# Moving the second half's convolution beside the first half's attention, with three projection panels taken out of that stage

## The chip, the cores and the metric

The kernel runs on one core of a Trainium2 chip. The metric is the device time of one launch in microseconds (us): the median of the runs of the kernel before is 1644.02 us, over three runs from 1640.84 to 1645.38. The profile is that of one further execution, with a time of 1639.46 us.

## The reference, cut to what matters

One layer of a decoder over 1024 tokens of width 1024, in float32, with three sub-layers. Only the parts that the change touches are written out.

```python
def reference(x, mem, ...):
    mem_n = rms_norm(mem, mem_norm_g)
    # 1. two mixers side by side, from one projection
    p = rms_norm(x, g[0]) @ w_in                       # 1024 -> 1024 + 1792 columns
    y_conv = conformer_conv(p[..., :1024])             # gate, causal conv of width 31, layer norm, silu
    y_rwkv = rwkv7_mix(p[..., 1024:])                  # token shift, then a recurrence over tokens
    x = x + rms_norm(concat([y_conv, y_rwkv]) @ w_out, g[1])
    # 2. attention of 4 heads into 256 memory tokens
    x = x + rms_norm(memory_cross_attention(rms_norm(x, g[2]), mem_n, wq, wkv, wo), g[3])
    # 3. channel mixer
    return x + rms_norm(swiglu(rms_norm(x, g[4]), w_gu, w_down), g[5])

def conformer_conv(u):
    h = u[..., :512] * sigmoid(u[..., 512:])
    h = causal_depthwise_conv(h, conv_w) + conv_b      # 31 taps per channel
    return silu(layer_norm(h, ln_g, ln_b))
```

## The kernel before, in words

**Halves.** The tokens are worked on in two halves of 512. `run` (from L955) writes the stages of half 0 (projection, mixers, attention), then those of half 1, with the channel mixer of half 0 as filler in half 1's stages, and last the channel mixer of half 1.

**Matmuls.** Every large product is made of three matmuls, of a high and a low part of each operand (`mm3`, L197). Each weight tile of 128x1024 is loaded into a ring of four `wraw` tiles (L177), ScalarE makes the high part `whi` (L171), and VectorE (or GpSimd where `pool_share` is above 0) makes the low part `wlo` (L172); `whi` and `wlo` have two tiles each, so weights are used in the order in which the program asks for them. `feat` (L203) makes one 128x512 tile `psf` with 24 matmuls; `tokmajor` (L212) makes four tiles `pst` at a time.

**Projection panels.** `w_in_block` (L300) takes a list of panels, each of two such `psf` tiles. The convolution's panels (4, 0, 6, 2) gate their columns and write them to `hd` in DRAM (L332). The other mixer's panels (20, 12, 8, 16, 14, 10, 18) go through `evq` (L311 to L324) to `pdr`.

**The convolution.** `conv_taps` (L341) loads 128 channels of `hd` into `hin` (two tiles), makes the first tap on ScalarE (L349) and thirty more: for three of the four channel groups on VectorE (L356), for group 0 with a product on ScalarE (L353) and a sum on GpSimd (L354). `conv_norm` (L361) is the layer norm and the silu, with the results written to `yd` (L398).

**Order.** The instructions of each engine stand in an order that is fixed when the program is built: a scheduler with costs of its own takes what is ready, what comes earlier in the program first, so a later instruction that is ready goes into a gap. `weave(main, side, rate)` (L53) puts steps of `side` between those of `main` in the program, in proportion to the numbers that both yield. `fill(us)` (L784) takes steps of `self.filler` until their numbers have used up the credit. In half 0, `self.filler` holds the seven mixer panels of half 1, and gets a credit of 6 at the load before the output projection, 6 for each of the four token tiles of a `residual` (L763), and 5 before the transposes of the attention; a step of it counts 5.2.

**Stages around the change.** In the mixers' stage of half 0 the recurrence's `rwkv_chain` is followed by `memory_maps` (L823), the norm of half 1, and half 1's convolution panels, woven with half 0's convolution. Then come `mix_out` and `attention` of half 0, with the panels as filler. After that half 1 has `rwkv_prep` (L422), `rwkv_inverse` (L592: 31 dependent steps, GpSimd for the first 20 rows and VectorE for the rest, L621 and L622), and `rwkv_chain` (L652); half 1's convolution is woven into the channel mixer of half 0 behind them (L1054). A `residual` with a next norm scales and adds (L772), squares on ScalarE (L253), takes a root on GpSimd (L239), scales again (L265), and `transposed` (L271) makes the pairs `nextT` that the next stage's matmuls read.

Of the kernel before, what the change touches and what calls it, by code (L numbers as in the profile page):

```python
# [9 lines left out]
F32 = mybir.dt.float32  # L10
F32R = mybir.dt.float32r
AF = mybir.ActivationFunctionType
# [5 lines left out]
P = 128  # L18
# [3 lines left out]
TB = 512  # L22
# [30 lines left out]
def weave(main, side, rate):  # L53

    lag = 0.0
    for us in main:
        yield us
        lag += us * rate
        while lag > 0.0:
            lag -= next(side, 1e9)  # L60
    drain(side)


def drain(*gens):
    for g in gens:
        for _ in g:
            pass


class Trunk:  # L70
    def __init__(self, ctx, tc, x, mem, cols, lora, gpost, w_in, w_out, wqT, wkv, wo, w_gu, w_down, out):
# [5 lines left out]
        nc = self.nc  # L77
# [46 lines left out]
        nc.gpsimd.memset(self.mhalf, -0.5)  # L124
        self.carry = cp.tile([P, 14], F32, name="carry")
        nc.gpsimd.memset(self.carry, 0.0)
        pad = cp.tile([P, 40], F32, name="pad")
        nc.gpsimd.memset(pad, 0.0)

        def derive(name, n, src, mul, add):  # L130
            t = cp.tile([P, n], F32, name=name)
            nc.vector.tensor_scalar(t, src, mul, add, op0=ALU.mult, op1=ALU.add)
            return t
        col = self.col
# [6 lines left out]
        nc.vector.tensor_scalar(self.cwh, self.cwh, 0.5, None, op0=ALU.mult)  # L141
        self.lgh = derive("lgh", 4, col("ln_g"), 0.5, 0.0)
        self.lbh = derive("lbh", 4, col("ln_b"), 0.5, 0.0)


        self.pool_share = self.share = 0.0
# [18 lines left out]
    def col(self, name, i=None, n=1):  # L165
        a, b = COLS[name]
        return self.cols[:, a:b] if i is None else self.cols[:, a + i:a + i + n]
# [172 lines left out]

    def conv_taps(self, b, pool, acc):  # L341
        nc = self.nc
        t0 = b * TB
        for j in CONV_ORDER:
            h = pool.tile([P, 576], F32, tag="hin", bufs=2, name="hin")[:, 0:TB + CONVW - 1]
            nc.sync.dma_start(out=h, in_=self.hd[j * P:(j + 1) * P, t0:t0 + TB + CONVW - 1])
            a = acc[:, j, :]
            w = lambda k: self.cwh[:, j * CONVW + k:j * CONVW + k + 1]
            nc.scalar.activation(out=a, in_=h[:, 0:TB], func=AF.Identity, scale=w(0), bias=self.col("conv_b", j))  # L349
            for k in range(1, CONVW):  # L350
                if j == CONV_POOL:
                    p = pool.tile([P, TB], F32, tag="t", bufs=2, name="tap")
                    nc.scalar.activation(out=p, in_=h[:, k:k + TB], func=AF.Copy, scale=w(k))  # L353
                    nc.gpsimd.tensor_tensor(out=a, in0=a, in1=p, op=ALU.add)  # L354
                else:
                    nc.vector.scalar_tensor_tensor(out=a, in0=h[:, k:k + TB], scalar=w(k), in1=a,  # L356
                                                   op0=ALU.mult, op1=ALU.add)
                if k % 6 == 0:
                    yield 4.0

    def conv_norm(self, b, pool, acc):  # L361
        nc = self.nc
        t0 = b * TB
        tmp = lambda name: pool.tile([P, TB], F32, tag="t", bufs=2, name=name)
        add = lambda out, x, y: nc.vector.tensor_tensor(out=out, in0=x, in1=y, op=ALU.add)
        sa, sb = tmp("lnsa"), tmp("lnsb")
        add(sa, acc[:, 0, :], acc[:, 1, :])
        add(sb, acc[:, 2, :], acc[:, 3, :])
        add(sa, sa, sb)
        ps = self.pn.tile([P, TB], F32, tag="n", name="psln")  # L370
        nc.tensor.matmul(ps, self.ones, sa, start=True, stop=True)
        for j in range(4):
            nc.vector.scalar_tensor_tensor(out=acc[:, j, :], in0=ps, scalar=-1.0 / DR, in1=acc[:, j, :],
                                           op0=ALU.mult, op1=ALU.add)
        yield 6.0
        sa = tmp("lnsq")
        nc.scalar.activation(out=sa, in_=acc[:, 0, :], func=AF.Square)
        for j in range(1, 4):
            sb = tmp("lnsq")
            nc.scalar.activation(out=sb, in_=acc[:, j, :], func=AF.Square)  # L380
            add(sb, sa, sb)
            sa = sb
        ps = self.pn.tile([P, TB], F32, tag="n", name="psln2")
        nc.tensor.matmul(ps, self.ones, sa, start=True, stop=True)
        rs = pool.tile([P, TB], F32, tag="hin", bufs=2, name="lnrs")
        nc.vector.tensor_scalar(rs, ps, 1.0 / DR, LN_EPS, op0=ALU.mult, op1=ALU.add)
        ry = pool.tile([P, TB], F32, tag="hin", bufs=2, name="lnry")
        self.rsqrt(ry, rs, pool.tile([P, TB], F32, tag="t", bufs=2, name="lnt"))
        yield 6.0
        for j in range(4):  # L390
            a = acc[:, j, :]
            nc.vector.tensor_tensor(out=a, in0=a, in1=ry, op=ALU.mult)
            th = pool.tile([P, TB], F32, tag="t", bufs=2, name="lnth")
            sc, bi = self.lgh[:, j:j + 1], self.lbh[:, j:j + 1]
            nc.scalar.activation(out=th, in_=a, func=AF.Tanh, scale=sc, bias=bi)
            nc.scalar.activation(out=a, in_=a, func=AF.Identity, scale=sc, bias=bi)
            nc.vector.scalar_tensor_tensor(out=a, in0=th, scalar=1.0, in1=a, op0=ALU.add, op1=ALU.mult)
            nc.sync.dma_start(out=self.yd[j * P:(j + 1) * P, t0:t0 + TB], in_=a)  # L398
            yield 2.0
# [555 lines left out]
    def run(self):  # L955
        tc = self.tc
        L, R = "left", "right"
        opened = {}

        def push(name, side):  # L960
            opened[name] = tc.tile_pool(name=name, bufs=1, side=side, reuse_waits="tile")
            return opened[name].__enter__()

        def pop(*names):
            for n in names:
                opened.pop(n).__exit__(None, None, None)
# [5 lines left out]
        conv_cols, mix_cols = (4, 0, 6, 2), (20, 12, 8, 16, 14, 10, 18)  # L972
# [5 lines left out]
        ev = push("ev", R)  # L978
        mk = push("mk", R)
        a0 = push("a0", R)  # L980
        h0, h1, mT = self.pairs(a0), self.pairs(a1), self.pairs(mk, MEM, "m")
# [22 lines left out]
        kp = push("conv0", L)  # L1004
# [10 lines left out]
        def next_norm():  # L1015
            for t in range(0, 4, 2):
                self.normed(self.x, TB, (t, t + 2), h1, "g_mix", 2, (self.pd, "d"))
                yield 1.0 * 2
        maps = self.memory_maps(mT, ev, kv)
        w1 = self.w_in_block(1, h1, ev, conv_cols)  # L1020
        main = chain(islice(maps, 16), next_norm(), islice(w1, 0), maps, w1)
        drain(weave(main, self.conv(0, kp), 1.0))
        pop("mix0", "gn0", "conv0", "tt0", "xb", "kv", "mk")
        self.filler = self.w_in_block(1, h1, ev, mix_cols)

        yp = push("y0", L)
        a2 = push("a2", L)
        self.xn = 3
        self.xp = push("xc", R)
        ap = push("pc", R)  # L1030
        drain(self.mix_out(0, a2, yp))
        drain(self.attention(0, self.nextT, a2, yp, ap))
        self.fill(1e9)
        pop("pc", "xc")
        pop("ev", "a1")

        ya, ss = self.ya_tiles(yp), self.sums()
# [4 lines left out]
        pop("prep1")  # L1042
        tp = push("tt1", R)
        TT = tp.tile([P, NCH * HP, CH], F32, tag="TT", name="TT")
        kp = push("conv1", R)
        pp = push("inv1", R)
        self.rwkv_values(1, pp)
        self.rwkv_inverse(1, pp, TT)
# [1 line left out]
        gp = push("gn1", R)  # L1050
        mp = push("mix1", R)
        self.rwkv_chain(1, mp, gp, TT)
        side = self.conv(1, kp)
        self.filler = weave(self.filler, side, 1.5)  # L1054
        self.fill(270.0)
        drain(side)
        pop("mix1", "gn1", "conv1", "tt1")
        self.pool_share = 0.3
        a3 = push("a3", R)
        y1 = push("y1", R)  # L1060
# [2 lines left out]
        ap = push("pd1", R)  # L1063
# [72 lines left out]
```

## Time and profile before

| what | value |
|---|---|
| median of three runs | 1644.02 us (1640.84 to 1645.38) |
| profiled execution: its own time | 1639.46 us |
| profiled execution: its span, first to last instruction | 1637.7 us |
| mean granted clock of TensorE | 0.966 |
| TensorE matmul busy | 1537.0 us, 94% of the span |
| VectorE, ScalarE, GpSimd busy | 1056.9, 721.7, 369.3 us |

"Busy" is the share of time in which an engine has at least one instruction under way. For TensorE it does not say how fast it works: its granted clock is 1.0 (2.4 GHz) or 0.5 (1.2 GHz), and a stretch's mean tells how long it stood at the lower level. So a stretch's loss on TensorE is read as its idle time, plus the length times (1 - clock).

### The profile page before, as it was taken

The numbers are of one execution on the slowest core, as the hardware profiler recorded it, in microseconds if no ns is written. First come the engines' busy times: TensorE is split into PE (matmuls) and PEld (weight loads), VectorE is DVE, ScalarE is ACT, GpSimd is POOL, SyncE is SP. The second block draws the span as 40 slices with busy tenths as digits, with TensorE's granted clock in tenths as the row PEclk, the third lists the DMA queues.
The fourth block names the chain that finished last, engine by engine and source line by source line (L and its number), as shares of the span: only waits on it lengthen the run. The fifth ranks groups of instructions, "written<-read, shape, count | busy, mean of one in ns | idle before, by whom it ended". The sixth has DMA issues, their size and how long they took to land.

```text
span 1637.7 us, 22825 instructions
## 1 busy us (share of the span) xinstructions
PE 1537.0 (94%) x8688; PEld 1256.5 (77%) x8688; DVE 1056.9 (65%) x1501; ACT 721.7 (44%) x1122; POOL 369.3 (23%) x347
## 2 busy tenths in 40 slices
PE   7999867879999999999979889999999999999997
PEld 6777756767787888777758667878887788888886
DVE  5687698997545546768789997536537624343435
ACT  5654335867434434654224555534435332222222
POOL 1032390740000000022561730012113211111111
PEclk9999976889999999999999889999999999999999
DMA  6576967466636236457844235446236632323221
GB/s 203 174 222 202 280 210 230 123 201 224 223 130 204 96 109 191 143 161 225 245 129 136 94 113 168 136 141 206 90 94 230 229 101 92 103 90 103 90 90 52
DMA packets 175644, 257.37 MB, mean 157 GB/s; under 512 B 68912, under 2 KB 110000, under 8 KB 175536
## 3 DMA queue, kind: packets, MB, share of 16 engines
q1 hardware_dynamic: 174576, 255.08, 49.1%
q8 instruction: 68, 1.11, 0.3%
q10 hardware_dynamic: 960, 0.85, 0.2%
q14 instruction: 40, 0.33, 0.1%
HBM read 196.58 MB, written 59.31 MB: 156 GB/s over the span
## 4 chain that ended last, share of the span: by engine, by line
PE 44%; DVE 5%; POOL 4%; issue 2%; DMA 1%; ACT 1%; SPq 0%; POOLq 0%; DVEq 0%; ACTq 0%
PE psf L201 7%; PE psf L199 7%; PE psf L200 7%; PE pst L199 6%; PE pst L200 6%; PE pst L201 6%; DVE acc L356 2%; POOL tm L621 1%; POOL Tt L622 1%; DVE wlo L172 1%; PE psg L528 1%; DMA At<-sc 0%; DVE ya L921 0%; POOL rstd L239 0%; POOL wlo L172 0%
## 5 line engine op out<-in xcount | busy, mean ns | idle before, releaser
L171 ACT CAST whi<-wraw 128x1024 fp32r<-128x1024 f32 x256 | 268.0, 1049 | 533.8 <-PE psf L200 182.6
L201 PE MATMUL psf<-ahi,wlo 128*128 128x512 f32 (+1 forms) x1200 | 462.6, 386 | 26.2 <-DVE wlo L172 25.1
L199 PE MATMUL psf<-ahi,whi 128*128 128x512 f32 (+1 forms) x1200 | 460.7, 385 | 8.1 <-ACT whi L171 8.1
L200 PE MATMUL psf<-alo,whi 128*128 128x512 f32 (+1 forms) x1200 | 460.3, 384 | 0.0
L172 DVE TENSOR_TENSOR wlo<-wraw,whi 128x1024 fp32r<-128x1024 f32 x223 | 285.9, 1283 | 253.4 <-ACT whi L171 251.9
L201 PEld LDWEIGHTS psf<-ahi,wlo 128*128 128x128 f32 x1200 | 231.5, 193 | 74.7 <-DVE wlo L172 30.3
L199 PEld LDWEIGHTS psf<-ahi,whi 128*128 128x128 f32 x1200 | 231.7, 193 | 53.0 <-ACT whi L171 10.0
L200 PEld LDWEIGHTS psf<-alo,whi 128*128 128x128 f32 x1200 | 231.8, 193 | 42.7 <-issue 1.2
L172 POOL TENSOR_TENSOR wlo<-wraw,whi 128x1024 fp32r<-128x1024 f32 x33 | 79.8, 2417 | 554.4 <-ACT whi L171 497.6
L356 DVE SCALAR_TENSOR_TENSOR acc<-hin,cols,acc 128x512 f32<-128x512 f32 x180 | 164.3, 941 | 0.7
L200 PE MATMUL pst<-wlo,ahi 128*128 128x512 f32 x384 | 150.2, 391 | 1.4 <-POOL wlo L172 0.9
L201 PE MATMUL pst<-whi,alo 128*128 128x512 f32 x384 | 148.4, 391 | 0.0
L199 PE MATMUL pst<-whi,ahi 128*128 128x512 f32 x384 | 135.6, 395 | 2.5 <-ACT ahi L282 2.1
L200 PE MATMUL pst<-wlo,fhi 128*128 128x512 f32 x352 | 137.8, 392 | 0.1
L201 PE MATMUL pst<-whi,flo 128*128 128x512 f32 x352 | 134.3, 390 | 0.0
L199 PE MATMUL pst<-whi,fhi 128*128 128x512 f32 x352 | 134.0, 393 | 0.0
L239 POOL TENSOR_TENSOR rstd<-rstd,mhalf 128x1 f32<-128x1 f32 x50 | 34.5, 699 | 386.2 <-DVE rstd L238 376.9
L354 POOL TENSOR_TENSOR acc<-acc,tap 128x512 f32<-128x512 f32 x60 | 99.4, 1656 | 85.6 <-ACT tap L353 82.0
L921 DVE TENSOR_TENSOR ya<-pst,ya 128x512 f32<-128x512 f32 x80 | 54.3, 687 | 51.9 <-PE pst L201 51.8
L199 PEld LDWEIGHTS pst<-whi,ahi 128*128 128x128 f32 x384 | 71.6, 188 | 18.2 <-ACT ahi L282 2.6
L200 PEld LDWEIGHTS pst<-wlo,ahi 128*128 128x128 f32 x384 | 72.1, 188 | 16.8 <-POOL wlo L172 1.2
L201 PEld LDWEIGHTS pst<-whi,alo 128*128 128x128 f32 x384 | 71.8, 188 | 14.5
(244 smaller groups left out, 2006.5 us busy)
## 6 DMA issues: line engine op xcount, KB each, us to landing
wraw<-in_w_gu_dram SPq DMA_DIRECT2D x88, 512.0 KB, 3.6
wraw<-in_w_in_dram SPq DMA_DIRECT2D x44, 512.0 KB, 4.5
wraw<-in_w_down_dram SPq DMA_DIRECT2D x44, 512.0 KB, 3.6
wraw<-in_wkv_dram SPq DMA_DIRECT2D x16, 512.0 KB, 5.1
am<-amd SPq DMA_DIRECT2D x16, 512.0 KB, 5.3
wraw<-in_w_out_dram SPq DMA_DIRECT2D x16, 512.0 KB, 4.1
wraw<-gd SPq DMA_DIRECT2D x16, 512.0 KB, 4.4
wraw<-vwd SPq DMA_DIRECT2D x16, 512.0 KB, 3.4
```

What stands on the lines that cost most here:

```text
L171: self.nc.scalar.copy(out=hi, in_=src)
L172: (eng or self.nc.vector).tensor_tensor(out=lo, in0=src, in1=hi.bitcast(F32), op=ALU.subtract)
L199: mm(ps, w[0], x[0], start=start, stop=False)
L200: mm(ps, w[0], x[1], start=False, stop=False)
L201: mm(ps, w[1], x[0], start=False, stop=stop)
L239: nc.gpsimd.tensor_tensor(r, r, self.mhalf, op=ALU.pow)
L354: nc.gpsimd.tensor_tensor(out=a, in0=a, in1=p, op=ALU.add)
L356: nc.vector.scalar_tensor_tensor(out=a, in0=h[:, k:k + TB], scalar=w(k), in1=a, op0=ALU.mult, op1=ALU.add)
L528: nc.tensor.matmul(pg[g][:, i, :], bk[half[g], c + i, :], aq[half[g], :, c + i, :], start=True, stop=True)
L621: eng.tensor_tensor(out=w, in0=a, in1=c, op=ALU.mult)
L622: eng.tensor_tensor(out=u, in0=u, in1=w, op=ALU.add)
L921: nc.vector.tensor_tensor(out=y, in0=ps, in1=y, op=ALU.add)
```

## The change

- Half 1's convolution is written beside `mix_out` and `attention` of half 0, as the side of a `weave` with a rate of 0.7, and no longer behind half 1's `rwkv_chain`. Its pool `conv1` is opened on the right after `pc`, and closed with it.
- Its bias columns come from a new tile `cb` (128x8: `conv_b`, and the halved bias of the layer norm) in the constant pool, with one slot under the tag `convb`. Half 0's copy is made at the start by two VectorE copies; half 1's copy is made by two ScalarE copies at the head of `conv_taps(1)`, and its slot comes free with the last instruction of half 0's convolution that reads the bias (L395 and L396). The first tap (L349) of half 1 needs it. The `pad` tile shrinks by the same eight columns.
- The first three mixer panels of half 1 (20, 12, 8) are written behind the convolution's panels in the mixers' stage; the filler of the attention stage keeps four panels (16, 14, 10, 18). An `islice(w1, 0)` that took nothing goes.
- The filler in half 1's chain stage is now the channel mixer alone, with the same credit of 270.

```diff
+        self.cb = cp.tile([P, 8], F32, tag="convb", name="convb0")
+        nc.vector.tensor_copy(out=self.cb[:, 0:4], in_=col("conv_b"))
+        nc.vector.tensor_copy(out=self.cb[:, 4:8], in_=self.lbh)
...
     def conv_taps(self, b, pool, acc):
+        if b == 1:
+            self.cb = self.cp.tile([P, 8], F32, tag="convb", name="convb")
+            nc.scalar.copy(out=self.cb[:, 0:4], in_=self.col("conv_b"))
+            nc.scalar.copy(out=self.cb[:, 4:8], in_=self.lbh)
...
-            nc.scalar.activation(out=a, in_=h[:, 0:TB], func=AF.Identity, scale=w(0), bias=self.col("conv_b", j))
+            nc.scalar.activation(out=a, in_=h[:, 0:TB], func=AF.Identity, scale=w(0), bias=self.cb[:, j:j + 1])
...
-            sc, bi = self.lgh[:, j:j + 1], self.lbh[:, j:j + 1]
+            sc, bi = self.lgh[:, j:j + 1], self.cb[:, 4 + j:5 + j]
...
-        main = chain(islice(maps, 16), next_norm(), islice(w1, 0), maps, w1)
+        w1m = self.w_in_block(1, h1, ev, mix_cols[:3])
+        main = chain(islice(maps, 16), next_norm(), maps, w1, w1m)
...
-        self.filler = self.w_in_block(1, h1, ev, mix_cols)
+        self.filler = self.w_in_block(1, h1, ev, mix_cols[3:])
...
-        drain(self.mix_out(0, a2, yp))
-        drain(self.attention(0, self.nextT, a2, yp, ap))
+        kp = push("conv1", R)
+        def blocks():
+            yield from self.mix_out(0, a2, yp)
+            yield from self.attention(0, self.nextT, a2, yp, ap)
+        drain(weave(blocks(), self.conv(1, kp), 0.7))
         self.fill(1e9)
...
         self.rwkv_chain(1, mp, gp, TT)
-        side = self.conv(1, kp)
-        self.filler = weave(self.filler, side, 1.5)
         self.fill(270.0)
-        drain(side)
```

## Rows read from the trace of the kernel before

**Rows 1.** Busy us, share, instructions; granted clock in tenths, 40 slices

```profile
PE 1537.0 (94%) x8688; PEld 1256.5 (77%) x8688; DVE 1056.9 (65%) x1501; ACT 721.7 (44%) x1122; POOL 369.3 (23%) x347
...
PEclk9999976889999999999999889999999999999999
```

**Rows 2.** By stretch: length, then PE, PEld, DVE, ACT, POOL busy; clock; DMA

```profile
800.00:825.00 25.00, 23.09 (x106) 18.73 (x104) 24.79 (x43) 6.77 (x9) 22.96 (x26) 1.00 0.68 240
825.00:850.00 25.00, 17.07 (x72) 12.90 (x70) 20.08 (x21) 5.34 (x7) 20.67 (x28) 0.98 0.30 95
850.00:875.00 25.00, 24.22 (x367) 18.94 (x368) 24.00 (x34) 11.76 (x20) 0.00 (x0) 0.89 0.58 134
875.00:900.00 25.00, 25.00 (x203) 20.02 (x202) 21.39 (x33) 9.69 (x14) 4.44 (x3) 1.00 0.50 159
900.00:925.00 25.00, 20.75 (x147) 16.24 (x145) 24.79 (x21) 13.43 (x22) 18.40 (x13) 0.93 0.25 80
925.00:950.00 25.00, 19.42 (x109) 14.83 (x107) 24.83 (x24) 17.27 (x26) 20.08 (x12) 0.82 0.35 106
950.00:975.00 25.00, 21.50 (x132) 16.75 (x131) 24.38 (x32) 9.05 (x16) 6.72 (x5) 0.84 0.44 137
975.00:1000.00 25.00, 25.00 (x186) 19.56 (x185) 19.32 (x31) 17.37 (x25) 0.00 (x0) 1.00 0.35 111
...
1350.00:1375.00 25.00, 25.00 (x112) 20.71 (x111) 9.43 (x10) 6.53 (x9) 2.39 (x1) 1.00 0.30 101
```

**Rows 3.** The same view, of half 0's attention stage and of the GpSimd taps

```profile
410.00:690.00 280.00, 278.18 (x1290) 227.55 (x1289) 155.28 (x256) 126.74 (x209) 11.36 (x21) 1.00 0.48 156
...
895.00:957.00 62.00, 51.10 (x349) 39.67 (x347) 61.09 (x54) 38.31 (x58) 49.60 (x30) 0.89 0.30 93
```

**Rows 4.** VectorE's groups from 850 to 895 us: count, busy us, mean ns, idle before

```profile
L356 DVE SCALAR_TENSOR_TENSOR acc<-hin,cols,acc 128x512 f32<-128x512 f32 x36 | 25.1, 743 | 0.0
L172 DVE TENSOR_TENSOR wlo<-wraw,whi 128x1024 fp32r<-128x1024 f32 x7 | 8.5, 1221 | 7.9 <-ACT whi L171 7.9
```

**Rows 5.** The same view from 895 to 957 us, VectorE and then GpSimd

```profile
L356 DVE SCALAR_TENSOR_TENSOR acc<-hin,cols,acc 128x512 f32<-128x512 f32 x24 | 30.9, 1290 | 0.4
L172 DVE TENSOR_TENSOR wlo<-wraw,whi 128x1024 fp32r<-128x1024 f32 x5 | 10.1, 2013 | 0.0
...
L742 DVE TENSOR_TENSOR Y<-Y,yrr 128x512 f32<-128x512 f32 x1 | 1.8, 1778 | 0.0
...
L937 DVE SCALAR_TENSOR_TENSOR ftg<-ftg,psf 128x512 f32<-128x512 f32 x2 | 1.3, 674 | 0.0
...
L354 POOL TENSOR_TENSOR acc<-acc,tap 128x512 f32<-128x512 f32 x30 | 49.6, 1655 | 59.6 <-ACT tap L353 57.6
```

**Rows 6.** Who waited for whom, 790 to 865 us: total, times, longest

```profile
ACT Tn L625 <- POOL Tt L622: 10.4, 1, 10.4
...
PE psf L199 <- ACT whi L171: 5.4, 1, 5.4
```

**Rows 7.** The inverse's sums on GpSimd; half 1's taps: min/median/max ns, first and last start

```profile
L622 POOL TENSOR_TENSOR Tt<-Tt,tm x31: 250/657/1504, 796.7 to 847.5; 128x60 f32<-128x60 f32 x2, 128x220 f32<-128x220 f32 x2, 128x240 f32<-128x240 f32 x2, 128x247 f32<-128x247 f32 x2
...
L356 DVE SCALAR_TENSOR_TENSOR acc<-hin,cols,acc x90: 735/746/1829, 809.4 to 965.9; 128x512 f32<-128x512 f32 x90
```

**Rows 8.** The panels' evictions from 608 to 656 us: ns, first and last start

```profile
L311 ACT ACTIVATE evq<-psf,omu x7: 676/682/684, 616.3 to 651.8; 128x512 f32<-128x512 f32 x7
```

**Rows 9.** VectorE in order of time behind the attention: start us, us, idle before

```profile
609.54 1.28 DVE L772 SCALAR_TENSOR_TENSOR ya<-ya,rstd,xres 128x1024 f32<-128x1024 f32 x1
...
630.49 0.75 DVE L265 TENSOR_SCALAR ya<-ya,rstd 128x1024 f32<-128x1024 f32 x1 [0.60 <-POOL rstd L239]
```

**Rows 10.** TensorE in order of time there: last product of the attention

```profile
609.72 0.39 PE L201 MATMUL pst<-whi,alo 128*128 128x512 f32 x1
```

**Rows 11.** Half 1's gated columns written, and the convolution's last bias reader

```profile
L331 DVE SCALAR_TENSOR_TENSOR evh<-tg,psf x4: 679/680/681, 403.5 to 431.1; 128x512 f32<-128x512 f32 x4
...
L396 ACT ACTIVATE acc<-acc,lbh,lgh x4: 798/803/816, 400.7 to 406.3; 128x512 f32<-128x512 f32 x4
```

More of the change, by code (lines that the diff above doesn't have):

```diff
@@ L126, in __init__ @@
         nc.gpsimd.memset(self.carry, 0.0)
-        pad = cp.tile([P, 40], F32, name="pad")
+        pad = cp.tile([P, 32], F32, name="pad")
         nc.gpsimd.memset(pad, 0.0)
@@ L1030, in run @@
         ap = push("pc", R)
-        drain(self.mix_out(0, a2, yp))
-        drain(self.attention(0, self.nextT, a2, yp, ap))
+        kp = push("conv1", R)
[3 more added lines that the diff above has]
+        drain(weave(blocks(), self.conv(1, kp), 0.7))
         self.fill(1e9)
-        pop("pc", "xc")
+        pop("conv1", "pc", "xc")
         pop("ev", "a1")
@@ L1044, in run @@
         TT = tp.tile([P, NCH * HP, CH], F32, tag="TT", name="TT")
-        kp = push("conv1", R)
         pp = push("inv1", R)
@@ L1052, in run @@
         self.rwkv_chain(1, mp, gp, TT)
-        side = self.conv(1, kp)
-        self.filler = weave(self.filler, side, 1.5)
         self.fill(270.0)
-        drain(side)
-        pop("mix1", "gn1", "conv1", "tt1")
+        pop("mix1", "gn1", "tt1")
         self.pool_share = 0.3
```

## The prediction, made before the change was run

> **What bounds the kernel now.** I read the busy time first: TensorE is busy for 94% of the span, and its granted clock is below full only around slices 6 to 9 and 23 to 24 [rows 1]. So the time is TensorE's work plus what it loses, and a change that moves other engines' work is worth what TensorE loses in one place less what it loses in the other. The view by stretch gives the losses, as idle time plus length times (1 - clock). In a steady stretch 112 matmuls of 512 columns pass in 25 us without loss, 0.223 us each (1350 to 1375 us) [rows 2], so a `psf` of 24 takes 5.4 us. Half 1's taps on VectorE run from 809 to 966 us [rows 7]. In these stretches the loss is 1.9, 8.4 and 3.5 us from 800 to 875, 0 from 875 to 900, 6.0, 10.1 and 7.5 us from 900 to 975, and 0 after that, where the chain goes on with no taps [rows 2]: 13.8 us beside the inverse and 23.6 us in the chain. Half 0's attention, where the convolution is put, loses next to nothing: TensorE is busy for 278.2 of 280 us at full clock, VectorE for 155.3, GpSimd for 11.4 [rows 3].
>
> The view by lines then tells why the taps cost what they cost. From 850 to 895 us VectorE runs 36 taps of 743 ns each without a break, GpSimd does nothing, and TensorE loses little [rows 2, 4]. From 895 to 957 us GpSimd makes its 30 sums of channel group 0, VectorE has not 1 us to spare, and its taps take 1290 ns, its `wlo` 2013 instead of 1221 ns [rows 3 to 5]. Taps alone are cheap; taps beside GpSimd's sums are not.
>
> **What goes.** (1) The chain stage, 23.6 us. Without the convolution VectorE has there what it has from 975 us on (19.3 of 25 us busy, loss 0), so nearly all comes back. I leave 2 us for the chain's own hops: 21.5 us, between 17 and 23.6. The matmuls of the filler that stay are the same, by the same credit.
> (2) The inverse, 13.8 us from 800 to 875. Its end holds up ScalarE's copy `Tn` for 10.4 us, `whi` queues behind that copy, and TensorE waits 5.4 us for it [rows 6]. GpSimd's steps reach 1504 ns there at a median of 657 [rows 7], and the taps begin in the midst of them; without taps I expect the steps to be shorter and most of the loss to go: 9 us, between 5 and 13.
> Together 30.5 us, between 22 and 36.6.
>
> **What comes.** (3) The convolution beside the attention. VectorE gets 90 taps of 0.74 us and some 21 instructions of the norm of about 0.68 us (as the `psf` reader's 674 ns [rows 5]): 81 us, on 140 of 280 us (155.3 less, by my estimate, 15 for half 1's preparation, which begins at the end of that stretch [rows 3]). ScalarE, with 126.7 of 280 us busy, has room for 30 products and some 20 instructions more. That fits, as long as GpSimd's sums don't stretch it. From 895 to 957 us they did: 24 taps x 0.547 = 13.1, 5 `wlo` x 0.792 = 4.0, and the chain's own two-input work, by my estimate nine or ten instructions' worth at about 1.1 (1778 against some 690 ns), 10: some 27 us for 30 sums, or 0.9 us a sum [rows 4, 5]. The attention has taps and `wlo` but no chain: at least 13.1 + 4.0 = 17 us, at most 27; I take 20. TensorE lost 23.6 us for those 27 by 975 us, and 10.9 + 0.11 x 62 = 17.7 us within 895 to 957 [rows 2, 3], so 0.66 to 0.88 per us: 13 to 18 us. As scores and outputs need only `wlo` and an eviction in time, and no hops of a chain, I take 15. The ends: 0, where VectorE's free half hides it all, and 24, where the price moves with the taps.
>
> Here a rule has to be weighed. While GpSimd adds, the VectorE instructions that read PSUM keep their 674 ns; those with two inputs in SBUF stretch [rows 5]. The Trainium skill says the same (SBUF — State Buffer, section "SBUF: two separate sides"): the port pair of the two engines is an exclusive lock for a whole instruction, for a VectorE instruction with two SBUF inputs against one of GpSimd's that reads SBUF. At the ceiling of that lock, where each sum blocks VectorE for its whole 1655 ns [rows 5], 30 sums take 50 us from it, term (3) is 33 in place of 15, and the sum +19.5, 1663 us. The rows show 0.9 us a sum, and they decide.
>
> (4) The held tile. Its two ScalarE copies wait for the last bias reader, which is ScalarE's own (L396, start 406.3 us) [rows 11], so what is queued behind them (`whi`, evictions) waits for nothing that it did not wait for already. Two copies of 4 columns at the start and two here: 0, at most 1 us. Half 1's gated columns are written from 403.5 to 431.1 us [rows 11], so the taps can begin near 413 us, in VectorE's gaps, and GpSimd's sums once one `hin` is free, by my estimate near 460 to 480 us; before that the taps stand alone, as in rows 4. The loads of `hin` and the writes of `yd` go through SP's queue with the weights' loads; late taps delay those, which is inside the 0.66 to 0.88.
>
> (5) The three panels. Their six `psf`, 6 x 5.4 = 32 us of TensorE, leave the attention stage and go to the end of the mixers' stage, where TensorE has no idle time to fill: 0 by themselves. But they were cover. Of the 14 panel tiles seven are evicted only behind the attention's last product [rows 8], which ends at 610.1 us [rows 10]. What hides behind those seven is the second `residual`: four rounds of scale, add, square, root and scale, the first at 609.5, the last at 630.5 us and over at 631.2 [rows 9], some 21 us; then a transpose and a copy, 1 us. The channel mixer's first matmul needs that result. The credit counts by steps of 5.2: two tiles for the load, four in the first `residual`, one before the transposes, and the eighth in the second `residual`. With 14 tiles that left seven, as seen; with 8 it leaves one, 5.4 us. Half 1's preparation can't fill in: its tiles take the place of `h1` and `ev`, which the eighth tile still reads. So TensorE stands from about 615.5 to between 629 (rounds of 4.6 us by my estimate, with less to share the engines with) and 632 us: 14 to 16.5 us, and one or two more at 1.2 GHz, as behind the idle time at 825 to 850 us [rows 2]. I take 16, between 9 and 20. This is new; the first `residual` keeps its four tiles.
> (6) Late rounds in that first `residual`, if taps stand between its steps: 1, between 0 and 5.
>
> **The sum.** -21.5 - 9 + 15 + 0 + 16 + 1 = +1.5 us on the profiled execution's 1639.46 us, hence 1641.0; the median of the runs is 4.56 us above that execution, so 1645.5, say 1646 us.
>
> **Rivals.**
> A, the forecast: gains and new losses about cancel; 1636 to 1655 by (3) and (5) within 5 us of what I took. For it: each term has a row. Chance 0.42.
> B, faster: the attention absorbs the taps. Its VectorE is half idle and much of its work reads PSUM, which GpSimd doesn't slow [rows 3, 5]; then (3) is 3 and (6) 0, and the sum is -21.5 - 9 + 3 + 16 = -11.5: 1632 us. If the rounds also get shorter (5 at 9), 1625. Against it: the scheduler packs taps into every gap, so where the sums run, VectorE may be as full as at 895 us. Chance 0.30.
> C, slower: GpSimd's sums meet VectorE's taps and the first `residual` in the attention at the old price. Place: the 50 to 60 us of the sums; price 24, and 5 for (6); the sum is -30.5 + 24 + 16 + 5 = +14.5: 1658 us. It decides slower from (3) + (6) of 20 us on (30.5 - 16 + 5). For it: the same 30 sums and 90 taps, and an order of instructions made beforehand, which can't step aside. Against: no chain. With a full block by each sum, as weighed under (3), it would be 1668, 0.03 of the chance. Chance 0.23.
> D, the change doesn't do what it says: the convolution's tiles on the right come free only late, so its end runs into the second `residual` and the preparation. Then (3) is small, but (5) and (6) grow; 1640 to 1660, 1650. Nothing in the rows shows it. Chance 0.05.
>
> **How the numbers follow.** A measurement here tells 0.3% from no change, 5 us either way: 1639 to 1649. A spreads over it with about 0.05 faster, 0.24 same, 0.13 slower; B 0.28 faster, 0.02 same; C 0.22 slower, 0.01 same; D 0.01, 0.01, 0.03. Sum: faster 0.34, same 0.28, slower 0.38. The range reaches from between B's two ends to past C: 1628 to 1662. A alone has 1636 to 1655.
>
> **What would show it.** (1) The stretches between half 1's inverse and its `mix_out` with TensorE at full clock and no idle time. (2) GpSimd's inverse steps over in clearly less than the 51 us of before [rows 7], and `Tn` waiting less. (3) Taps above 1 us and clock below 1.0 where GpSimd's sums stand, before the first `residual`; with taps of 743 ns and a full clock there B is right. (5) A gap of 14 us or more on TensorE between the eighth panel tile and the channel mixer's first `psf`; no gap there makes the forecast too high by 16 us. It is wrong in its core if the taps still stand in the chain, or if the loss of the attention stage is below 10 us in all.

## The result: slower by 1.2%, and where the time went

The changed kernel takes 1664.94 us (median of four runs, 1660.80 to 1665.20) against 1644.70 us of the kernel before in the same job: a ratio of 1.0121, with a 95% interval from 1.0097 to 1.0145, some 20 us more. The forecast was 1646 us in a range from 1628 to 1662; the time lies 3 us above that range.

| profiled execution | before | after |
|---|---|---|
| its own time, us | 1639.46 | 1665.19 |
| mean granted clock of TensorE | 0.966 | 0.959 |
| TensorE, VectorE, GpSimd busy, us | 1537.0, 1056.9, 369.3 | 1545.1, 1054.5, 359.5 |

The engines' work is the same [rows 1]; only its place differs. The page's first and second part, after:

```profile
PE 1545.1 (93%) x8688; PEld 1258.9 (76%) x8688; DVE 1054.5 (63%) x1503; ACT 722.2 (43%) x1124; POOL 359.5 (22%) x347
...
PEclk9999975989998899889999999999999999999999
```

The dip of slices 23 and 24 is gone, and slices 13, 14, 17 and 18 (500 to 580 and 665 to 750 us) are new. By stretch, after (length, then PE, PEld, DVE, ACT, POOL busy, clock, DMA):

```profile
425.00:450.00 25.00, 22.18 (x86) 17.80 (x85) 19.79 (x28) 12.22 (x16) 0.00 (x0) 0.86 0.40 133
450.00:475.00 25.00, 24.63 (x109) 20.07 (x108) 25.00 (x44) 10.78 (x16) 0.00 (x0) 1.00 0.72 242
...
500.00:525.00 25.00, 20.00 (x80) 16.07 (x81) 24.80 (x23) 12.85 (x23) 19.64 (x13) 0.93 0.30 96
525.00:550.00 25.00, 18.27 (x73) 14.36 (x72) 24.68 (x21) 13.80 (x24) 18.84 (x13) 0.86 0.20 63
550.00:575.00 25.00, 21.63 (x85) 17.24 (x84) 24.21 (x33) 10.59 (x16) 12.70 (x9) 0.86 0.61 211
575.00:600.00 25.00, 19.51 (x88) 14.72 (x87) 18.92 (x33) 11.57 (x18) 2.79 (x3) 0.86 0.45 147
...
425.00:625.00 200.00, 174.44 (x728) 138.87 (x726) 179.28 (x248) 100.49 (x156) 57.92 (x38) 0.92 0.43 140
675.00:750.00 75.00, 60.54 (x249) 46.87 (x248) 49.29 (x68) 39.60 (x61) 9.28 (x14) 0.86 0.42 135
...
700.00:725.00 25.00, 19.43 (x79) 15.01 (x80) 13.14 (x19) 11.76 (x19) 1.27 (x4) 0.73 0.28 89
...
800.00:900.00 100.00, 96.59 (x485) 77.60 (x483) 66.61 (x101) 32.62 (x43) 49.28 (x75) 1.00 0.76 224
900.00:1075.00 175.00, 174.33 (x1512) 139.11 (x1513) 93.08 (x139) 77.06 (x117) 0.00 (x0) 1.00 0.47 138
```

And before, the stretch that has no row yet:

```profile
675.00:750.00 75.00, 73.58 (x372) 57.47 (x371) 55.87 (x71) 43.97 (x61) 14.77 (x12) 1.00 0.53 155
```

Read them as idle time of TensorE plus length times (1 - clock). From 900 to 1075 us the loss is 0.7 us, where half 1's chain lost 23.6 [rows 2]. From 800 to 900 us it is 3.4 us, where the inverse lost 13.8 [rows 2]. From 425 to 625 us it is 25.6 + 200 x 0.08 = 41.6 us, where the whole attention stage lost 1.8 [rows 3]. From 675 to 750 us it is 14.5 + 75 x 0.14 = 25.0 us, where the kernel before lost 1.4 us. So 33.3 us were gained and 63.4 lost, +30. The profiled execution is 25.7 us longer than that of before, not 20, because the latter is 5 us below its median. The other 4 us stand in stretches that I did not take apart; 1.3 of them are idle time of the kernel before from 975 to 1075 us, which the 23.6 leave out.

Beside the sums, after, VectorE's and GpSimd's groups by shape from 480 to 562 us (count, busy us, mean ns, idle before):

```profile
L364 DVE SCALAR_TENSOR_TENSOR acc<-hin,cols,acc 128x512 f32<-128x512 f32 x47 | 54.0, 1156 | 0.7
L175 DVE TENSOR_TENSOR wlo<-wraw,whi 128x1024 fp32r<-128x1024 f32 x11 | 19.7, 1789 | 0.1
L811 DVE TENSOR_TENSOR ya<-pst,gb 128x512 f32<-128x512 f32 x8 | 5.4, 678 | 0.0
L780 DVE SCALAR_TENSOR_TENSOR ya<-ya,rstd,xres 128x1024 f32<-128x1024 f32 x1 | 2.3, 2308 | 0.0
```
```profile
L362 POOL TENSOR_TENSOR acc<-acc,tap 128x512 f32<-128x512 f32 x30 | 50.0, 1668 | 146.8 <-ACT tap L361 145.0
```

These answer to [rows 5]: the same 30 sums, taps at 1156 ns where they take 743 without sums, `wlo` at 1789 where it takes 1221 [rows 4], and the reader of PSUM at 678 (674 in [rows 5]). Who waited for whom, after, 425 to 640 us (total, times, longest):

```profile
ACT acc L357 <- DMA hin<-hd: 20.1, 4, 6.7
PE pst L203 <- DVE wlo L175: 8.3, 2, 6.6
DVE acc L364 <- ACT acc L357: 6.9, 1, 6.9
PE psf L204 <- DVE wlo L175: 6.6, 3, 3.4
PE pst L202 <- DVE ss L817: 4.9, 1, 4.9
PE psln L379 <- DVE lnsa L373: 4.6, 1, 4.6
```

TensorE waits for low parts of weights (14.9 us), for VectorE's step on a norm's sum of squares (`ss`, 4.9 us), and for the convolution's own layer norm (4.6 us): `psln` has its fixed place among TensorE's matmuls, and what is behind it stands too. For the rounds of the first `residual` (`ya`, L268) it waits only 0.6 us: they start from 562.4 to 582.8 us, and the last sum starts at 561.0 us. The start is told by VectorE and ScalarE in order of time (start us, us, idle before):

```profile
420.53 1.23 DVE L175 TENSOR_TENSOR wlo<-wraw,whi 128x1024 fp32r<-128x1024 f32 x1 [0.55 <-ACT whi L174]
428.68 3.11 DVE L364 SCALAR_TENSOR_TENSOR acc<-hin,cols,acc 128x512 f32<-128x512 f32 x4 [6.92 <-ACT acc L357]
...
432.97 1.22 DVE L175 TENSOR_TENSOR wlo<-wraw,whi 128x1024 fp32r<-128x1024 f32 x1
```
```profile
427.83 0.82 ACT L357 ACTIVATE acc<-hin,convb,cols 128x512 f32<-128x512 f32 x1 [6.70 <-DMA hin<-hd]
428.55 1.03 ACT L174 CAST whi<-wraw 128x1024 fp32r<-128x1024 f32 x1
```

The first tap holds ScalarE 6.7 us for the load of its columns, with `whi` behind it; VectorE stands 6.9 us for the first tap, with four taps and then `wlo` behind. The second `residual` is told by TensorE's last panel tile and what follows:

```profile
691.61 0.39 PE L204 MATMUL psf<-ahi,wlo 128*128 128x512 f32 x1
691.85 0.49 PE L282 MATMUL pstr<-ident,ya 128*128 128x128 f32 x3
696.89 0.90 PE L282 MATMUL pstr<-ident,ya 128*128 128x128 f32 x3 [4.55 <-DVE ya L268]
702.70 0.90 PE L282 MATMUL pstr<-ident,ya 128*128 128x128 f32 x3 [4.91 <-DVE ya L268]
705.85 0.90 PE L282 MATMUL pstr<-ident,ya 128*128 128x128 f32 x3 [2.25 <-DVE ya L268]
707.37 1.22 PE L202 MATMUL psf<-ahi,whi 128*128 128x512 f32 x2 [0.63 <-ACT ahi L285]
```

From 691.9 to 707.4 us only transposes run, and three times they wait for a round of the norm.

### The profile page after: what moved, and what is told of

It reads as the page before. It is cut to its first block, busy times and chain, and to the rows that moved or that the text cites. A ratio compares the mean times of both kernels' runs of the same rounds, so it can differ in the third digit from the quotient of the medians.

```text
span 1663.4 us, 22827 instructions
## 1 busy us (share of the span) xinstructions
PE 1545.1 (93%) x8688; PEld 1258.9 (76%) x8688; DVE 1054.5 (63%) x1503; ACT 722.2 (43%) x1124; POOL 359.5 (22%) x347
## 4 chain that ended last, share of the span: by engine, by line
PE 64%; DVE 12%; ACT 4%; POOL 4%; issue 3%; DMA 2%; SPq 0%; DVEq 0%; POOLq 0%; ACTq 0%
PE psf L204 11%; PE psf L202 11%; PE psf L203 11%; PE pst L202 9%; PE pst L203 9%; PE pst L204 9%; DVE acc L364 4%; DVE wlo L175 3%; POOL tm L629 2%; POOL Tt L630 1%; ACT whi L174 1%; PE pstr L282 1%; DVE ya L780 1%; DMA hin<-hd 1%; PE psg L536 1%
## 5 line engine op out<-in xcount | busy, mean ns | idle before, releaser
L175 DVE TENSOR_TENSOR wlo<-wraw,whi 128x1024 fp32r<-128x1024 f32 x223 | 290.6, 1304 | 255.7 <-ACT whi L174 254.7
L948 DVE SCALAR_TENSOR_TENSOR ftg<-ftg,psf 128x512 f32<-128x512 f32 x44 | 30.1, 686 | 87.5 <-PE psf L204 87.4
```

Of the source, the lines that this page charges most:

```text
L175: (eng or self.nc.vector).tensor_tensor(out=lo, in0=src, in1=hi.bitcast(F32), op=ALU.subtract)
L948: nc.vector.scalar_tensor_tensor(out=tg, in0=tg, scalar=0.5, in1=pu, op0=ALU.mult, op1=ALU.mult)
```

## The experiments

The theory after the result: the loss has two causes that don't depend on each other, the GpSimd sums beside a VectorE that the taps have filled, and the missing cover behind the second `residual`. Rivals: the taps alone, the held bias tile, ScalarE's wait for the load.

**e1: the sums left out.** The kernel after, without half 1's 30 sums on GpSimd (so channel group 0 of its convolution has the first tap alone); ScalarE's products stay.

```diff
-                    nc.gpsimd.tensor_tensor(out=a, in0=a, in1=p, op=ALU.add)
+                    if b == 0:
+                        nc.gpsimd.tensor_tensor(out=a, in0=a, in1=p, op=ALU.add)
```

> The changed kernel, with GpSimd's 30 sums of channel group 0 left out in half 1's convolution (their ScalarE products stay). The changed kernel's median is 1664.9 us; between 425 and 675 us TensorE loses about 41 us (idle time plus length times (1 - clock)), 24 of them from 500 to 575 us, beside the sums. Theory collision: the sums stretch VectorE's taps and wlo, and that makes TensorE late. Then the loss from 500 to 575 falls below 6 us, part of the 9 us behind it goes too, taps take 743 ns throughout, and the time is 1635 to 1645 us. Theory load: VectorE is full there with 90 taps whoever else works; then the loss stays above 15 us and the time above 1655 us.

Measured: 1639.32 us, ratio to before 0.9979 (0.9965 to 0.9993). The sums are worth 1.42% of the time, 23 us; the time lies in the range of theory collision. By stretch, e1, and its waits for low parts from 425 to 625 us:

```profile
425.00:625.00 200.00, 191.45 (x843) 153.36 (x842) 168.03 (x281) 109.52 (x183) 7.78 (x8) 0.98 0.47 152
625.00:675.00 50.00, 39.77 (x176) 32.21 (x174) 24.29 (x38) 18.32 (x33) 4.67 (x9) 0.93 0.49 162
675.00:750.00 75.00, 71.03 (x323) 55.52 (x324) 55.16 (x69) 41.42 (x61) 8.70 (x9) 0.91 0.45 135
```
```profile
PE psf L204 <- DVE wlo L175: 2.8, 3, 1.8
PE pst L203 <- DVE wlo L175: 1.1, 2, 0.6
```

From 425 to 625 us the loss is 8.6 + 4 = 12.6 us: 29 of the 41.6 were the sums' (17 idle time, 12 clock), and 11 more than before stay with the rest of the convolution: its taps, products, loads and layer norm, which this run doesn't tell apart. TensorE's waits for low parts fall from 14.9 to 3.9 us and those for `ss` from 4.9 to 0.2; the taps take 746 ns. From 500 to 575 us the loss is 7.2 us, where below 6 was expected. The gap behind the second `residual` stays (10.2 + 3.5 and 4.0 + 6.8, 24.4 us), only earlier: it does not come from the sums.

**e2 and e3: the panels alone, from both sides.** e2 is the kernel after with all seven panels as filler of the attention again; e3 is the kernel before with nothing changed but the three panels' place.

```diff
# e2, against after
-        w1m = self.w_in_block(1, h1, ev, mix_cols[:3])
+        w1m = self.w_in_block(1, h1, ev, mix_cols[:0])
-        self.filler = self.w_in_block(1, h1, ev, mix_cols[3:])
+        self.filler = self.w_in_block(1, h1, ev, mix_cols[0:])
```
```diff
# e3, against before
+        w1m = self.w_in_block(1, h1, ev, mix_cols[:3])
-        main = chain(islice(maps, 16), next_norm(), islice(w1, 0), maps, w1)
+        main = chain(islice(maps, 16), next_norm(), islice(w1, 0), maps, w1, w1m)
-        self.filler = self.w_in_block(1, h1, ev, mix_cols)
+        self.filler = self.w_in_block(1, h1, ev, mix_cols[3:])
```

> The changed kernel with all seven mixer panels left to the filler, none in the mixers' stage. Theory cover: the about 23 us that TensorE loses from 675 to 750 us come from the missing panel tiles behind the attention's second residual. Then that loss falls below 6 us and the time is 1644 to 1650 us. Rival: the six panel tiles, back in the attention stage, meet the taps there (each has a wlo, an eviction and two sums on VectorE) and cost as much as they cover; then the attention stage loses 10 us more than 41 and the time is 1655 to 1665 us.

> The kernel before with the three panels moved alone; the convolution stays behind the chain. Theory cover: TensorE stands 14 us or more behind the attention's second residual, as worked out beforehand, and the time is 16 to 21 us above the kernel before, 1660 to 1666 us. Rival: the gap is closed by other work, or given back in the chain stage, where half 1's preparation is ready earlier; then it is within 6 us of the kernel before.

Measured: e2 1653.65 us, ratio 1.0054 (1.0032 to 1.0077); e3 1663.51 us, ratio 1.0124 (1.0106 to 1.0143). By stretch, e2 (with its longest wait of TensorE from 420 to 600 us) and then e3:

```profile
425.00:625.00 200.00, 168.37 (x718) 134.19 (x717) 181.19 (x257) 103.10 (x171) 56.87 (x38) 0.91 0.40 133
...
675.00:750.00 75.00, 75.00 (x352) 60.34 (x350) 51.55 (x72) 41.59 (x58) 10.42 (x8) 1.00 0.46 136
```
```profile
PE pstr L282 <- DVE ya L268: 16.7, 2, 8.9
```
```profile
425.00:625.00 200.00, 198.31 (x902) 163.06 (x901) 102.21 (x181) 81.92 (x143) 4.61 (x8) 1.00 0.47 150
625.00:675.00 50.00, 37.00 (x165) 29.58 (x163) 27.02 (x42) 21.25 (x37) 4.66 (x9) 0.86 0.50 163
```

In e3 the three panels alone cost 1.24%, 20 us: the attention is as before (1.7 us lost), and the gap behind it loses 13.0 + 7.0 us; the time is as theory cover has it. In e2 the gap is gone (0 from 675 to 750 us), but the gain is 0.67%, 11 us, for the attention loses 49.6 in place of 41.6 us. (By these stretches the gain is 17 us, and so it is in the profiled execution, the fastest of five at 1647.99 us.) With six panel tiles fewer ahead of the stage, the first `residual` comes earlier: its rounds (L268) start from 509.3 to 543.2 us, among the sums (484.6 to 551.2). L268 takes 1746 ns in the median there, 752 in the kernel after, and TensorE waits 16.7 us for `ya`. In this the two causes do touch. So the cover is not worth its whole price, as theory cover has it, and the time lies between the two expectations. That the returning panels' own work on VectorE costs as much as they cover, as the rival has it, isn't shown.

**e4 and e5: the sums turned into taps.** e4 is the kernel after with half 1's channel group 0 on VectorE like the others, so 120 taps and no sum; e5 is e4 with the seven panels of e2.

```diff
-                if j == CONV_POOL:
+                if j == CONV_POOL and b == 0:
```

> The changed kernel with half 1's channel group 0 on VectorE as the other three groups: 30 more taps there, no ScalarE products and no GpSimd sums in half 1. Theory collision: 30 taps of 0.66 to 0.75 us are 20 to 22 us more on VectorE, which had some 45 us left between 425 and 690 us; the 24 us beside the sums go, and the time is 1640 to 1650 us. Theory load: VectorE, already full from 450 to 575 us, makes TensorE later still, and the time is 1665 to 1685 us.

> The changed kernel without the move of the panels and with half 1's channel group 0 on VectorE: the edits of the second and of the fourth run together. Theory by stages: the panels' move costs 20 us behind the second residual wherever the convolution stands, the sums cost what GpSimd collides, and they add; then the loss behind the residual is below 3 us, the attention stage loses about 22 us as in the run with all taps on VectorE, and the time is 1628 to 1636 us, below the kernel before (1643.4). Rival: the stages trade, as the run with the panels back already showed (43 us lost in the attention, in place of 35): the attention stage loses 30 us or more and the time is 1638 to 1648 us.

Measured: e4 1652.12 us, ratio 1.0055 (1.0037 to 1.0072); e5 1637.31 us, ratio 0.9970 (0.9955 to 0.9984). By stretch, e4 and then e5:

```profile
425.00:625.00 200.00, 182.49 (x798) 147.39 (x797) 175.91 (x296) 83.26 (x141) 9.49 (x8) 0.96 0.44 143
...
550.00:575.00 25.00, 13.45 (x56) 10.62 (x57) 24.80 (x41) 8.31 (x14) 2.99 (x3) 0.73 0.37 126
```
```profile
425.00:625.00 200.00, 181.65 (x784) 145.94 (x783) 179.31 (x297) 88.05 (x151) 9.01 (x8) 0.94 0.42 137
...
675.00:750.00 75.00, 73.57 (x358) 59.12 (x357) 52.19 (x72) 41.65 (x61) 10.55 (x8) 1.00 0.50 153
```

```profile
L364 DVE SCALAR_TENSOR_TENSOR acc<-hin,cols,acc 128x512 f32<-128x512 f32 x120 | 86.2, 748 | 8.1 <-ACT acc L357 7.6
```

e4's taps (the last line) take 748 ns in the mean, not 959 as after from 425 to 625 us, so GpSimd's sums, and not the taps' number, had stretched them. 16 of the 41.6 us come back, though VectorE makes 30 taps more; theory collision had 24 and a time of at most 1650 us, 2 us too low. What stays is 25.5 us, of which 11.6 + 6.8 = 18.3 in one stretch, 550 to 575 us: there the first `residual`'s rounds stand between taps (TensorE waits 11.6 us for `ya`, L268). The two mends add up in the time: e5 gains 1.51% of the time before on after, against 0.66 + 0.67, and is a little faster than before. The time lies between the ranges of theory and rival: the gap is gone as in the theory (1.4 us lost), and the attention loses 30.4 us as in the rival, again with a wait for `ya` (9.3 us). The profiled execution is the slowest of ten, 1641.70 us, so 30.4 is rather too high.

**e6: the held tile.** The kernel after without half 1's own bias tile.

```diff
-            self.cb = self.cp.tile([P, 8], F32, tag="convb", name="convb")
-            nc.scalar.copy(out=self.cb[:, 0:4], in_=self.col("conv_b"))
-            nc.scalar.copy(out=self.cb[:, 4:8], in_=self.lbh)
```

> The changed kernel without the second allocation of the bias tile: half 1's convolution uses half 0's tile and isn't held back. In the changed kernel half 0's last bias reader ends near 407 us and the first load of half 1's taps is issued at 422 us, behind its input. If the input holds the taps in any case, the tile changes only the order a little and the time is within 5 us of the changed kernel, 1660 to 1670 us. If the tile holds them, they start earlier than 425 us, beside half 0's own last sums, the stretch to 430 us loses 5 us more, and the time is above 1670 us.

Measured: 1663.20 us, ratio 1.0118 (1.0088 to 1.0147), no different from after. As expected, the shared tile costs nothing that can be measured and holds back nothing that counts.

**e7 and e8: taps behind the first `residual`.** e7 is e5 with the last two channel groups held until the last norm of the first `residual` is written, through a bias tile made from it (0 x row + bias). e8 is e7 with half 1's first taps on GpSimd in place of ScalarE.

```diff
# e7, against e5
+            cb = self.cb2 if b == 1 and g >= 2 else self.cb
...
+                if b == 0 and gi == 0 and t == 3:
+                    self.cb2 = self.cp.tile([P, 8], F32, tag="convb2", name="convb2")
+                    nc.vector.scalar_tensor_tensor(out=self.cb2, in0=ya[3][:, 0:8], scalar=0.0, in1=self.cb,
+                                                   op0=ALU.mult, op1=ALU.add)
```
```diff
# e8, against e7
+            if b == 1:
+                nc.gpsimd.tensor_scalar(a, h[:, 0:TB], w(0), cb[:, j:j + 1], op0=ALU.mult, op1=ALU.add)
```

> As the run with the panels back and all taps on VectorE, but the third and fourth group of half 1's taps are held until the last norm of the first residual, by a bias tile that VectorE makes from it (0 times a row, plus the bias). Theory: what is left of the loss in the attention stage comes from taps between the serial steps of the first residual (with all taps on VectorE TensorE lost 18 us from 550 to 575 us, where it waited 11.6 us for the residual's rows, and next to nothing from 450 to 550). Then that loss falls to below 5 us and the time is 10 to 15 us below the same kernel without the hold, 1618 to 1626 us. Rival: taps shifted behind the residual meet the softmax and the second residual, and the time is within 5 us of the same kernel without it.

> As the run with the hold at the first residual, with half 1's four first taps made by GpSimd instead of ScalarE. In the changed kernel ScalarE stands 20 us before its first taps for the loads of hin, with whi queued behind them, and TensorE loses 6 us from 425 to 450 us. If that queue is the cause, TensorE is without loss there and the time is 4 to 8 us below the run before it; if VectorE's wlo or the load itself is, it is the same within 2 us.

Measured: e7 1633.06 us, ratio 0.9941 (0.9911 to 0.9971); e8 1634.12 us, ratio 0.9944 (0.9922 to 0.9967). The worse half of the first `residual`'s stretch, e5 and then e7:

```profile
525.00:550.00 25.00, 16.17 (x67) 12.82 (x68) 25.00 (x40) 7.12 (x11) 3.25 (x3) 0.73 0.33 117
```
```profile
525.00:550.00 25.00, 21.71 (x98) 17.66 (x99) 24.36 (x36) 10.88 (x15) 0.00 (x0) 0.93 0.25 83
```

The hold does what it should: the stretch with the first `residual` (500 to 550 us) loses 3.7 us idle and 1.8 by the clock, where e5 lost 9.6 and 6.8. TensorE waits 0.4 us for `ya`, in place of 9.3. But part of it comes back from 550 to 600 us (6.3 us lost, 3.8 in e5), where the held taps fill VectorE. The gain on e5 is 0.3%, within what the two intervals leave open: the time is the rival's, within 5 us of e5, and the larger gain that was expected did not come. e8 says that ScalarE's wait for the load is not what costs: without it, nothing changes. VectorE still waits 5.9 us there for the first tap, now on GpSimd.

**e9 and e10: the start.** e9 is e7 with the first two groups held too, until half 1's last gated tile is written; e10 is e7 again, beside it.

```diff
+                    if b == 1 and m == 3:
+                        self.cb1 = self.cp.tile([P, 8], F32, tag="convb1", name="convb1")
+                        nc.vector.scalar_tensor_tensor(out=self.cb1, in0=q[:, 0:8], scalar=0.0, in1=self.cb,
+                                                       op0=ALU.mult, op1=ALU.add)
...
-            cb = self.cb2 if b == 1 and g >= 2 else self.cb
+            cb = self.cb if b == 0 else self.cb1 if g < 2 else self.cb2
```

> The kernel e7 (seven panels as filler, half 1's channel group 0 on VectorE, groups 3 and 4 in order held behind the first residual) with the first two groups held too, until the last gated tile of half 1 is written (near 442 us). What is tested: in e7 VectorE stands 6.0 us at 426.5 us for the first tap, the first tap waits 5.8 us for the load of its columns, and behind it a run of four taps and then the low part of a weight are late; TensorE then stands 2.35 us and runs at half clock, 425 to 475 us losing 5.4 us idle and 5.0 us by the clock (50 x 0.10). Theory: VectorE's own wait for the first tap makes that loss; with the columns long there when the taps become due, 5 to 8 of the 10.4 us come back, and the ratio to before falls to 0.990 to 0.992. Rival: VectorE is simply full there, taps that start 15 us later push as much work into the stretch behind; the stretches 425 to 625 us lose within 3 us of what they lose in e7 and the ratio stays within 0.0015 of e7's.

> e7 word for word, beside e9 on the same chip and with the same runs of before: a ratio within 0.003 of the 0.9941 measured first, so 0.991 to 0.997; the theories of e9 are read from the two ratios of this job.

Measured: e9 1635.50 us, ratio 0.9960 (0.9946 to 0.9974); e10 1635.31 us, ratio 0.9957 (0.9941 to 0.9972). The rival holds. By stretch, e9 and then e10:

```profile
425.00:450.00 25.00, 21.61 (x93) 16.91 (x92) 21.78 (x35) 12.58 (x19) 0.00 (x0) 1.00 0.65 212
450.00:475.00 25.00, 24.34 (x107) 19.67 (x106) 25.00 (x41) 7.26 (x14) 0.00 (x0) 1.00 0.37 117
...
500.00:525.00 25.00, 15.94 (x69) 12.54 (x69) 18.52 (x35) 11.38 (x17) 2.67 (x5) 0.85 0.79 268
```
```profile
425.00:450.00 25.00, 21.86 (x89) 17.22 (x88) 22.45 (x32) 14.09 (x19) 0.00 (x0) 0.93 0.43 143
450.00:475.00 25.00, 22.66 (x92) 17.81 (x91) 25.00 (x40) 7.57 (x11) 0.00 (x0) 0.93 0.53 174
...
500.00:525.00 25.00, 23.21 (x108) 18.81 (x106) 17.92 (x33) 12.60 (x20) 4.06 (x7) 1.00 0.88 315
```

The loss of 425 to 475 us falls from 9.0 to 4.1 us, and 500 to 525 us loses 12.8 in place of 1.8; there TensorE waits 7.6 us for `ya`, 0.2 in e10. What the later taps give back at the start is lost again at the first `residual`.

No version is faster than e7, run twice: 0.4 to 0.6% faster than the kernel before, 1.6 to 1.8% faster than the changed one. e8 and e9 don't differ from it beyond the noise.

## Why the prediction was wrong, step by step

- **(1) The chain**, forecast -21.5: the loss fell from 23.6 to 0.7 us, -22.9. This was right in mechanism and size.
- **(2) The inverse**, forecast -9: from 13.8 to 3.4 us, -10.4. GpSimd's sums in it start within 42 us (855.0 to 896.8) in place of 51, their median is 537 in place of 657 ns [rows 7], and `Tn` waits 6.7 in place of 10.4 us [rows 6]. This was right too.
- **(3) The convolution beside the attention**, forecast +15 (0 to 24), with **(6)**, +1: this step failed. Together they measured 41.6 - 1.8 = +39.8 us. The mechanism held and three sizes did not. I estimated that the sums stretch VectorE by 17 to 27 us and took 20; they did by 47 x 0.41 for the taps, 11 x 0.57 for `wlo` and 1.0 for L780, 26.5 us. TensorE was to lose 0.66 to 0.88 us for each us of stretch, and I took 15 for 20, because there are "no hops of a chain". It lost 29 us for 26.5 (after against e1), 1.1 each: as waits for `wlo` (14.9 us, 3.9 in e1), for `ss` (4.9, 0.2 in e1) and, a little, for `psln` (4.6, 3.0 in e1), and 12 us by the clock. The attention has such waits of its own in place of the chain's hops; why a us of stretch costs more there than in the chain stays open. And the convolution without the sums, which I had priced at nothing because TensorE lost nothing from 875 to 900 us [rows 2, 4], cost 11 us (e1 against before). My sum of VectorE's work (140 of 280 us) was an average; beside the taps VectorE is busy for at least 24.2 of every 25 us from 450 to 575 us, with `wlo` queued behind them. Term (6), late rounds of the first `residual`, is hardly there in the changed kernel (0.6 us of waiting), because the rounds come just behind the sums: that is luck, as e2 shows, where they meet and TensorE waits 16.7 us.
- **(4) The held tile**, forecast 0: 0 (e6). The sentence that what is queued behind the two copies waits for nothing new holds for the copies. It left out the first taps behind them: these wait for the loads of `hin`, 20.1 us on ScalarE and 6.9 on VectorE. By e8 and e9, against e7, this wait does not set the time by itself.
- **(5) The three panels**, forecast +16 (9 to 20): e3 alone gives +20 us, and the stretch after +23.6. The gap was seen as it came: one panel tile, then 15.4 us with nothing but transposes, forecast 14 to 16.5. The clock behind it was mis-sized: I took one or two us, and 675 to 750 us lost 10.5 so (0.73 from 700 to 725 us).

Rival C had the sign and the sums' meeting with the taps. Its price of 24 + 5 was still 11 us short of (3) and (6), and the meeting with the first `residual`, which it priced at 5, took place in one step only (the first L780, 2308 ns). B failed in the first 25 us beside the sums (6.8 us lost from 500 to 525 us).

While the sums run, VectorE is stretched by 26.5 us for 30 of them, 0.88 us a sum. The Trainium skill (SBUF — State Buffer, section "SBUF: two separate sides") calls the shared port pair an exclusive lock for a whole instruction; at that ceiling the stretch would be 50 us, by the sums' 30 x 1.67 us. The 1663 us worked out from it lie near the measured time by luck, not for its reason: the stretch is half of that, and the rest is what TensorE lost for each us of it, the convolution without the sums, and the clock behind the gap.

## What to carry to other kernels

Free time of an engine over a whole stage doesn't say that work can be moved there: ask what stands behind the moved instructions in the engine's fixed order (here the low parts of weights), and whether a serial part (a norm's rounds, as in e2 and e4) lies in the same stretch. Before work is taken out of a stage, look at what it was cover for, and price the gap with the lowered clock behind it. And a wait that is removed from a full engine can come up again further on: in e9 4.9 us fewer were lost from 425 to 475 us, and 11 more from 500 to 525.

## What was not expected of the hardware

- A gap of 15 us with only short transposes is followed by a granted clock of 0.73 from 700 to 725 us and 0.93 from 725 to 750 us (1.2 GHz for part of each); in all, 675 to 750 us lost 10.5 us by the clock on top of 14.5 us of idle time.
- Short stalls can go with a lower clock: after, 2.8 us of idle time from 425 to 450 us went with a clock of 0.86 there. In e9 3.4 us of idle time in the same stretch left it at 1.00. The traces differ in how the idle time falls: after, it is one stall of 2.82 us before 434.24 us, and the clock is 0.50 from 435 to 440 us; in e9 it is three stalls, the longest of 1.44 us. That this is the cause isn't tested.
- A load of `hin` took 2.6 to 7.2 us from issue to landing (median 4.0). The first tap of half 1 stood 6.7 us on ScalarE for one that took 5.9 us, and VectorE 6.9 us for that tap.
- Not only VectorE instructions with two inputs in SBUF stretch beside GpSimd's sums. The norm's scaling (L268, one 128x1024 input and a column) took 1746 ns in the median among the sums of e2, 752 behind those of the kernel after.
